# A planned schedule for a two-layer decoder trunk: weight loads placed by a rule of their own, new tables, and the last scalings as three tasks

## The chip, the cores and the metric

The kernel runs on one core of a Trainium2 chip. The metric is the device time of one execution in microseconds (us), lower is better. The core has a matrix engine (TensorE, PE in the rows; PEld are its weight loads), a vector engine (VectorE, DVE), a scalar engine (ScalarE, ACT), GpSimd (POOL) and SyncE (SP), which does no arithmetic and issues nearly all DMAs here. Each engine runs its own list of instructions in order and waits for the others through semaphores.

## The reference

Two layers over 256 tokens of width 1024, then a final RMSNorm, all in float32. Each layer is

```python
h = rms_norm(x, norm_g[layer])
proj = jnp.einsum('btd,dc->btc', h, w_in[layer])          # 1024 x 3584
sb_q, sb_k, sb_v, sb_g, mb_q, mb_k, mb_v, mb_g, mem_q, mem_g = jnp.split(proj, split_at, axis=-1)
o_sb = stick_breaking_attention(sb_q, sb_k, sb_v) * jax.nn.silu(sb_g)          # 6 heads of 64
o_mb = moba_attention(rotary(mb_q), rotary(mb_k), mb_v) * jax.nn.silu(mb_g)    # 6 heads; causal softmax at this length
mk, mv = jnp.split(rms_norm(mem, mem_norm_g[layer]) @ w_mem_kv[layer], 2, axis=-1)
o_mem = softmax_attention(mem_q, mk, mv) * jax.nn.silu(mem_g)                  # 4 heads, 256 memory tokens
x = x + jnp.concatenate([o_sb, o_mb, o_mem], axis=-1) @ w_out[layer]
```

Merging of heads is left out above. The weights of both layers are some 42 MB, and each is used once.

## The kernel before

**A planner writes the program.** The kernel is recorded by a small list scheduler (`Sched`). Every piece of work is a Python generator that yields requests `R(engine, need=..., alloc=...)`; the scheduler keeps a planned time for each engine, takes the request that can start first (priority breaks ties), and lets the generator emit its instructions. So the order on every engine is fixed when the program is built, from planned costs. On the chip an instruction waits only for its data and its buffers; the planned times are gone.

**Weights.** A layer's projections are pieces such as `sb_q`, `mb_k`, `mem_g`, `mk`, `mv` and the two halves `wo0`, `wo1` of the output projection; `ORDER` gives their sequence. A piece is cut into chunks of one to four K-tiles (`NK`, `NKP`). A chunk goes through three steps: a DMA on SP writes it into a ring `raw`; `hi_task` rounds it to a short float in `hl` (a CAST, nearly always ACT); `lo_task` subtracts to get the rest (`hl<-raw,hl`, DVE). PE then multiplies hi by hi, hi by lo and lo by hi, three matmuls, or two where the piece is in `DBL` (hi and lo side by side: one of double width and one). `KMAJ` pieces go through K outermost, the others finish one output chunk after another.

**What sets the order of the loads.** In the version before, the next load is emitted right after a `lo` step, as soon as the ring has room (`dma_room`).

**Attention.** Heads are taken in pairs. Scores are PE matmuls on 64 rows (`bank<-sb_k,sb_q`, `bank<-uT` for mb, `bank<-mem_k,mem_q`), here called row groups; `SCG` says which pairs go together. ACT and DVE make the weights `w`. The transposition goes by way of DRAM and is called a trip below: DVE transposes 32x32 blocks into `D`, SP dumps `D` to `Z` in DRAM and reads it back in another order (four DMAs, or eight for those in `HALVES`) into `F`, `T` or, for the rotated q and k of mb, `ga` and `uT`. The values are then applied by PE matmuls to 64 columns (`bank<-F,sb_v`, `bank<-T,mb_v`, `bank<-T,mv`): column groups, `PVG`. The rotation of mb (`rope_task`, then `rope_turn`) is one ACT copy `rn<-bank`, four small DVE operations on `ru` and `rn` and a transposition `D<-rn` for each of two halves of the tokens, before its trip.

**The end.** `out_task` scales each half of the tokens by its 1/rms in three parts, each followed by its store.

Of the kernel before, what the change touches and what calls it, by code (L numbers as in the profile page):

```python
# [9 lines left out]
BF = mybir.dt.bfloat16  # L10
AF = mybir.ActivationFunctionType
# [5 lines left out]
D = 1024  # L17
# [27 lines left out]
P_H0 = 28
P_RX = -442
P_M0 = -424
P_RM = 1289
P_M1 = -280
# [22 lines left out]
P_SILU = -378
SCG = (((("mb", 1), ("mb", 2), ("sb", 1)), (("mem", 0), ("mem", 1)), (("mb", 0),), (("sb", 2),), (("sb", 0),)),
       ((("mb", 0), ("sb", 1)), (("sb", 0), ("sb", 2)), (("mb", 2),), (("mem", 0), ("mem", 1)), (("mb", 1),)))
PVG = (((("mb", 1), ("sb", 1), ("sb", 0)), (("mb", 0), ("sb", 2)), (("mem", 0), ("mb", 2)), (("mem", 1),)),
       ((("mb", 1), ("mb", 2), ("sb", 0), ("mem", 1), ("mem", 0), ("sb", 1)), (("mb", 0), ("sb", 2))))
HOLD = 800.0
HALVES = [("F", 1, "sb", 2), ("F", 1, "mb", 0)]
CROWD = 2
SPARE1 = 4  # L80
# [3 lines left out]
DVE_W = -36995.9
AHEAD = 181
DVE_HI = 17839.2
SLACK_PE = 60.0
# [26 lines left out]
class Sched:  # L114
# [37 lines left out]
    def _avail(self, k, eng):  # L152
        r = k.req
        t = k.t
        if k.eng == eng:
            t += 0.0 if eng == "pe" else LAT_SAME
        elif k.eng:
            t += LAT_CROSS
        for n in r.get("need", ()):
            if n not in self.ready:  # L160
                return None
            t = max(t, self.ready[n])
        for tag in r.get("alloc", ()):
# [12 lines left out]
        return t + r.get("late", PE_LATE) if eng == "pe" and k.gen.__name__ != "main" else t  # L176
# [60 lines left out]
def hybrid_trunk(ctx: ExitStack, tc: tile.TileContext, x, mem, norm_g, w_in, w_mem_kv, w_out,  # L237
                 final_norm_g, xT, memT, gcols, consts, out):
    nc = tc.nc
# [3 lines left out]
    S = Sched()  # L243
# [38 lines left out]
    def act(out, in_, func=AF.Copy, **kw):  # L282
        c = 0.833 * _free(in_) + (50.0 if is_psum(in_) else 93.0)
        for a in ("scale", "bias"):
            if a in kw and not isinstance(kw[a], float):
                c += 93.0
        if "accum_out" in kw:
            c += 93.0
        if func == AF.Copy and not kw:
            nc.scalar.copy(out, in_)  # L290
        else:
            nc.scalar.activation(out, in_, func, **kw)  # L292
        S.op("act", c)
# [9 lines left out]
    def ts(out, a, s, op=OP.mult):  # L303
        nc.vector.tensor_scalar(out, a, s, None, op0=op)  # L304
        S.op("dve", 1.0417 * _free(out) + 65.0 if is_psum(a) else 0.52 * _free(out) + 130.0)
# [16 lines left out]
    xs = sb("xs", [128, 2, D])  # L322
# [6 lines left out]
    junk = sb("junk", [128, 512], BF)  # L329
# [71 lines left out]
    for l in range(DEPTH):  # L401
# [56 lines left out]
    rawp, hlp = places(RAWC), places(HLC)  # L458
# [655 lines left out]
    def out_task(t, nb):  # L1114
        r = ss[1, t][:, 7:8]
        yield from rstd(ss[1, t], nb, r)
        edge = (0, 512, 768, 1024) if nb == 3 else (0, 512, 1024)
        for eng, a, b, q in (("act", 640, D, nc.scalar if t else nc.sync), ("dve", 0, 256, nc.sync), ("dve", 256, 640, nc.sync)):
            yield R(eng, need=[("gain", n, t) for n in range(nb) if edge[n] < b and edge[n + 1] > a])
            s = xs[:, t, a:b]  # L1120
            if eng == "act":
                act(s, s, AF.Copy, scale=r)
            else:
                ts(s, s, r)
            q.dma_start(out_r[:, t, a:b], s)


    def main():
        hT, mT = Ts
        yield R("dve")  # L1130
        nc.vector.memset(junk, 0.0)
# [23 lines left out]
        for l in range(DEPTH):  # L1155
# [59 lines left out]
            if l == 0:  # L1215
                p = pieces["sb_qk", 0]
# [149 lines left out]
```

## Time and profile before

| | |
|---|---|
| three runs | 265.19, 265.92, 267.18 us; median 265.92 |
| the profiled execution | 265.58 us, of which the profile's span is 263.8 |
| busy | PE 97%, PEld 86%, DVE 85%, ACT 72%, POOL 2% |
| DMA | 67.05 MB, 254 GB/s on average |
| granted PE clock | 0.993 of full speed on average |
| chain that ended last | PE 87%, DMA 7%, ACT, DVE and SP 1% each |

Times in the rows are counted from the span's start. A row of the timeline has start, length, engine, line, operation, output<-input and the number of instructions merged into it. A matmul's length includes its latency; how much of PE it takes is read from the start of one to the start of the next. Line numbers are those of the kernel before; every operation is emitted by a helper, so the names of the tiles tell more than the line.

### The profile page before, as it was taken

The page shows a single profiled execution, that of the slowest core. Times are in us where ns is not written, and L with a number is a line of the kernel's source. Part 1 is how long each engine was busy: PE and PEld are TensorE (multiplying, and loading weights), DVE is VectorE, ACT ScalarE, POOL GpSimd, SP SyncE. Part 2 cuts the span into 40 slices and gives each one's busy share as a digit, 9 for nine tenths or more (in the row PEclk, how much of TensorE's full clock was granted, in tenths as well). Part 3 has the DMA queues.
Part 4 walks back from the last instruction along what each step waited for, and adds up shares of the span by engine and source line. Part 5 has one row for each costly group of instructions (what it writes and reads, how often), then busy time and mean ns, then how long its engine had stood idle before and what let it go on. Part 6 is the DMA issues. An engine that isn't in the chain of part 4 may idle for free.

```text
span 263.8 us, 4793 instructions
## 1 busy us (share of the span) xinstructions
PE 256.1 (97%) x1597; PEld 227.6 (86%) x1597; DVE 225.0 (85%) x517; ACT 190.2 (72%) x393; POOL 6.1 (2%) x18
## 2 busy tenths in 40 slices
PE   8999999999999999999999999999999999999990
PEld 5889999998899987878899998888898899787880
DVE  3878999999899999989799586999999995978353
ACT  4789995999698795967665272966897899356133
POOL 1002000000100000000000000000000000000000
PEclk9999999999999999999999999999999999999997
DMA  7999998989979999978955939599878996961004
GB/s 202 359 395 357 390 361 264 317 295 283 373 209 315 314 299 253 267 244 274 308 172 201 352 95 243 212 264 320 263 211 216 330 279 229 254 233 53 0 0 159
DMA packets 49880, 67.05 MB, mean 254 GB/s; under 512 B 4224, under 2 KB 41472, under 8 KB 49856
## 3 DMA queue, kind: packets, MB, share of 16 engines
q1 hardware_dynamic: 48912, 64.85, 77.4%
q0 software_dynamic: 512, 1.31, 1.7%
q10 hardware_dynamic: 432, 0.59, 0.7%
q8 instruction: 12, 0.20, 0.4%
q14 instruction: 12, 0.10, 0.1%
HBM read 57.29 MB, written 9.44 MB: 253 GB/s over the span
## 4 chain that ended last, share of the span: by engine, by line
PE 87%; DMA 7%; ACT 1%; SPq 1%; DVE 1%; issue 0%; DVEq 0%; ACTq 0%
PE bank L273 86%; DMA T<-Z 3%; DMA raw<-in_w_out_dram 3%; DMA raw<-in_w_in_dram 2%; PE bank L279 1%; SPq L1018 1%; ACT hl L290 1%; ACT junk L292 1%; DVE xs L296 1%; SPq L378 0%; DVE xs L304 0%; ACT ss L292 0%; DVE T L300 0%; DVEq L1362 0%; DVE ss L628 0%
## 5 line engine op out<-in xcount | busy, mean ns | idle before, releaser
L296 DVE TENSOR_TENSOR hl<-raw,hl 128x768 fp32r<-128x768 f32 (+5 forms) x107 | 99.6, 947 | 7.9 <-ACT hl L290 6.0
L273 PE MATMUL bank<-T,hl 128*128 128x256 f32 (+1 forms) x646 | 106.1, 322 | 0.2 <-DVE T L300 0.2
L273 PEld LDWEIGHTS bank<-T,hl 128*128 128x128 f32 x646 | 92.6, 189 | 11.7 <-issue 1.8
L290 ACT CAST hl<-raw 128x768 fp32r<-128x768 f32 (+5 forms) x105 | 85.3, 841 | 17.0 <-DMA raw<-in_w_in_dram 6.4
L273 PE MATMUL bank<-hl,T 128*128 128x384 f32 (+1 forms) x448 | 79.6, 335 | 0.0
L273 PEld LDWEIGHTS bank<-hl,T 128*128 128x128 f32 x448 | 76.5, 188 | 2.2 <-issue 0.3
L273 PE MATMUL bank<-hl,mxhi 128*128 128x512 f32 (+1 forms) x144 | 41.2, 367 | 0.0
L273 PEld LDWEIGHTS bank<-hl,mxhi 128*128 128x128 f32 x144 | 26.1, 189 | 4.9 <-issue 0.4
L273 PE MATMUL bank<-hl,mxlo 128*128 128x512 f32 (+1 forms) x72 | 26.3, 366 | 0.0
L877 DVE STREAM_TRANSPOSE D<-w 128x384 f32<-128x384 f32 (+1 forms) x32 | 19.2, 602 | 3.2 <-ACT w L292 2.9
L292 ACT ACTIVATE junk<-xs 128x512 bf16<-128x512 f32 (+1 forms) x12 | 7.3, 610 | 13.6 <-DVE xs L296 13.1
L273 PEld LDWEIGHTS bank<-hl,mxlo 128*128 128x128 f32 x72 | 13.6, 189 | 2.2
L292 ACT ACTIVATE T<-uT,gc 128x256 fp32r<-128x256 f32 x24 | 11.4, 506 | 2.7 <-DMA uT<-xT_dram 2.7
L810 DVE TENSOR_TENSOR_SCAN a<-a,a 128x256 f32<-128x256 f32 (+1 forms) x24 | 12.8, 539 | 0.1
L292 ACT ACTIVATE a<-bank 128x384 f32<-128x384 f32 x24 | 11.3, 483 | 1.6 <-DVE a L810 0.9
L292 ACT ACTIVATE w<-w,st 128x128 f32<-128x128 f32 (+1 forms) x24 | 10.7, 448 | 2.3 <-DVE st L830 2.2
L292 ACT ACTIVATE a<-a 128x384 f32<-128x384 f32 x24 | 11.8, 522 | 0.2
L300 DVE SCALAR_TENSOR_TENSOR T<-uT,gc,T 128x256 fp32r<-128x256 f32 x24 | 11.4, 476 | 0.6 <-ACT T L292 0.6
L304 DVE TENSOR_SCALAR w<-w,st 128x256 f32<-128x256 f32 (+1 forms) x40 | 11.2, 323 | 0.2
L296 DVE TENSOR_TENSOR xs<-bank,xs 128x512 f32<-128x512 f32 (+1 forms) x8 | 5.3, 656 | 6.6 <-PE bank L273 6.5
L292 ACT ACTIVATE w<-bank,st 128x256 f32<-128x256 f32 x16 | 7.4, 488 | 4.1 <-DVE st L843 4.1
L290 ACT COPY gT<-bank 128x256 f32<-128x256 f32 x10 | 3.6, 372 | 7.7 <-PE bank L273 7.7
(106 smaller groups left out, 218.6 us busy)
## 6 DMA issues: line engine op xcount, KB each, us to landing
raw<-in_w_in_dram SPq DMA_DIRECT2D x39, 384.0 KB, 4.8
Z<-D SPq DMA_DIRECT2D x16, 384.0 KB, 5.0
raw<-in_w_out_dram SPq DMA_DIRECT2D x8, 512.0 KB, 6.0
raw<-in_w_in_dram SPq DMA_DIRECT2D x18, 192.0 KB, 4.0
raw<-in_w_in_dram SPq DMA_DIRECT2D x6, 576.0 KB, 5.7
raw<-in_w_in_dram SPq DMA_DIRECT2D x13, 256.0 KB, 4.9
raw<-in_w_mem_kv_dram SPq DMA_DIRECT2D x6, 512.0 KB, 6.2
raw<-in_w_out_dram SPq DMA_DIRECT2D x4, 768.0 KB, 6.4
```

The source lines that it names most:

```text
L273: nc.tensor.matmul(out, lhsT=lhsT, rhs=rhs, start=start, stop=stop, **kw)
L279: nc.tensor.transpose(out, in_, idt)
L290: nc.scalar.copy(out, in_)
L292: nc.scalar.activation(out, in_, func, **kw)
L296: nc.vector.tensor_tensor(out, a, b, op=op)
L300: nc.vector.scalar_tensor_tensor(out, a, s, b, op0=op0, op1=op1)
L304: nc.vector.tensor_scalar(out, a, s, None, op0=op)
L810: nc.vector.tensor_tensor_scan(a[:, r0:r1], a[:, r0:r1], u[:, r0:r1], 0.0, OP.add, OP.add)
L877: nc.vector.transpose(o, w[:, :n * 128].rearrange("p (m j r) -> p m j r", j=4, r=32))
L1018: nc.sync.dma_start(Fv[32 * j:32 * j + 32, i0:i1], Zv.rearrange("(i r) (j e) -> j r i e", i=4, j=4)[j, :, i0:i1])
```

## The change

The weight loads get a task of their own. `load_task` emits load j when the ring has room and, in the plan, load j-6 has landed (`LOADS = 6`); its priority is ahead of everything (`P_LD`). This is a condition of the planner: it moves the DMA in SP's list, and adds no semaphore wait to it. Six loads (`SPLIT`) are issued as two DMAs of half the size. The tables are new: the sequence of pieces, their cuts (107 chunks become 125: layer 0 has 56 for 59, layer 1 has 69 for 48), which pieces are in `DBL` (`sb_g` of layer 0 comes in, `mem_q` of layer 0 goes out) and `KMAJ`, the groups of pairs, the priorities. The warm-up matmuls read a constant of ones that exists already in place of a tile that DVE cleared. `out_task` spawns its three scalings as tasks in place of emitting them one after another.

```diff
-KORD = ((2, 3, 0, 1, 4, 5, 6, 7), (4, 5, 6, 7, 0, 1, 2, 3))
+KORD = ((0, 1, 2, 3, 4, 5, 6, 7), (4, 5, 6, 7, 2, 3, 0, 1))
...
+SPLIT = (14, 30, 47, 49, 63, 78)
+LOADS = 6
+P_LD = -30388
...
-ORDER = (["sb_qk", "mb_k", "mem_q", "mb_q", "mk", "mb_v", "mv", "sb_v", "sb_g", "mb_g", "mem_g"], ["mk",
-         "mb_k", "mb_q", "mem_q", "sb_q", "sb_k", "mv", "mb_v", "mem_g", "mb_g", "sb_v", "sb_g"])
+ORDER = (["sb_qk", "mb_k", "mb_q", "mv", "mem_q", "sb_v", "mb_v", "mk", "sb_g", "mb_g", "mem_g"], ["mk",
+         "mb_q", "mb_k", "mem_q", "mv", "mem_g", "sb_k", "sb_q", "mb_v", "mb_g", "sb_v", "sb_g"])
...
-        for n in r.get("need", ()):
+        for n in (*r.get("need", ()), *r.get("after", ())):
...
         if j in SPLIT:
+            m = n // 2
+            dma(dst[:, one[0], one[1]], src[:, one[0], one[1]], None, q, now)
...
-            dma_room(S.cur.t)
+            if LOADS >= 20:
+                dma_room(S.cur.t)
+
+    def load_task():
+        while prog["dma"] < len(chunks):
+            j = prog["dma"]
+            yield R("sp", need=[("lo", max(rawp[j][1]))] if rawp[j][1] else [],
+                    after=[("raw", j - LOADS)] if j >= LOADS else [])
+            dma_chunk(S.cur.t)
...
     def out_task(t, nb):
         r = ss[1, t][:, 7:8]
         yield from rstd(ss[1, t], nb, r)
+        S.mark(("rstd", t))
+        for eng, a, b in (("dve", 0, 256), ("dve", 256, 640), ("act", 640, D)):
+            S.spawn(store_task(t, nb, r, eng, a, b), a // 256)
...
-        nc.vector.memset(junk, 0.0)
...
-            mm(acc[:, :n], junk[:, :128], junk[:, :n], True, True)
+            mm(acc[:, :n], nc.const_aps.tensor(1.0, [128, 128], BF), nc.const_aps.tensor(1.0, [128, n], BF), True, True)
```

Three places in layer 1 show what the new tables move. First PE, where the scores of two mb pairs are taken. Before, they stand alone (the two mem pairs have a row group of their own, one piece earlier):

```order
L273 MATMUL bank_94<-T_74,hl 128x256
L273 MATMUL bank_92<-uT 128x128
L273 MATMUL bank_90<-uT 128x128
L273 MATMUL bank_92<-uT 128x256
L273 MATMUL bank_90<-uT 128x256
L273 MATMUL bank_97<-uT 128x128
L273 MATMUL bank_93<-uT 128x128
L273 MATMUL bank_97<-uT 128x256
L273 MATMUL bank_93<-uT 128x256
L273 MATMUL bank_91<-T_74,hl 128x512
```

Of the change, PE at the same group, from the second mb pair on (the first stands just ahead):

```order
L277 MATMUL bank_94<-uT 128x128
L277 MATMUL bank_92<-uT 128x128
L277 MATMUL bank_94<-uT 128x256
L277 MATMUL bank_92<-uT 128x256
L277 MATMUL bank_93<-mem_k,mem_q 128x256
L277 MATMUL bank_95<-mem_k,mem_q 128x256
L277 MATMUL bank_93<-mem_k,mem_q 128x256
L277 MATMUL bank_95<-mem_k,mem_q 128x256
L277 MATMUL bank_91<-mem_k,mem_q 128x256
L277 MATMUL bank_97<-mem_k,mem_q 128x256
L277 MATMUL bank_91<-mem_k,mem_q 128x256
L277 MATMUL bank_97<-mem_k,mem_q 128x256
```

The two groups have become one, at the end of the piece `mem_g`. Ahead of it now stand `mb_q`, `mb_k`, `mem_q`, `mv` and `mem_g`; before, `mb_k`, `mb_q`, `mem_q`, `sb_q` and part of `sb_k`.

Second DVE, at the rotation of the mb piece that PE finishes last (before that is `mb_q`, now `mb_k`). `ru` and `rn` are the rotation's tiles, 117 and 118 those of the second half of the tokens, and `D_108` is what the trip takes. Before:

```order
L296 TENSOR_TENSOR hl<-raw,hl 128x768 x3
L296 TENSOR_TENSOR ru_118<-rn_117,cst 128x6x8
L296 TENSOR_TENSOR hl<-raw,hl 128x768
L296 TENSOR_TENSOR ru_118<-rn_117,cst 128x6x8
L296 TENSOR_TENSOR hl<-raw,hl 128x768
L296 TENSOR_TENSOR rn_117<-rn_117,cst 128x6x16
L296 TENSOR_TENSOR hl<-raw,hl 128x768
L296 TENSOR_TENSOR rn_117<-rn_117,ru_118 128x6x16
L296 TENSOR_TENSOR hl<-raw,hl 128x768
L300 SCALAR_TENSOR_TENSOR mem_q<-bank_95,mem_q 128x256
L300 SCALAR_TENSOR_TENSOR mem_q<-bank_96,mem_q 128x256
L986 STREAM_TRANSPOSE D_108<-rn_117 128x3x4x32
```

Of the change, DVE at the rotation of `mb_k`:

```order
L300 TENSOR_TENSOR ru_118<-rn_117,cst 128x6x8
L300 TENSOR_TENSOR hl<-raw,hl 128x256
L300 TENSOR_TENSOR rn_117<-rn_117,cst 128x6x16
L1004 STREAM_TRANSPOSE D_108<-rn_115 128x3x4x32
L300 TENSOR_TENSOR rn_117<-rn_117,ru_118 128x6x16
L300 TENSOR_TENSOR hl<-raw,hl 128x256
L1004 STREAM_TRANSPOSE D_108<-rn_117 128x3x4x32
L300 TENSOR_TENSOR hl<-raw,hl 128x256 x4
L300 TENSOR_TENSOR hl<-raw,hl 128x768
```

Four subtractions of 768 columns and two evacuations that stood between the second half's steps have gone behind the transposition; two subtractions of 256 columns remain.

Third SP, where the two mb trips of layer 1 are issued. `Z_112<-D_107` and `Z_113<-D_108` are the dumps of the first and the second piece, `uT<-Z` and `ga<-Z` the returns. Before:

```order
L1005 DMA Z_112<-D_107 128x768
L378 DMA raw<-in_w_in_dram 128x2x384
L378 DMA raw<-in_w_mem_kv_dram 128x4x256 x2
L1018 DMA uT<-Z_112 32x4x192 x4
L378 DMA raw<-in_w_in_dram 128x3x384 x2
L1005 DMA Z_113<-D_108 128x768
L1018 DMA ga_114<-Z_113 32x4x192 x4
L378 DMA raw<-in_w_in_dram 128x2x384
L1005 DMA Z_111<-D_107 128x1024
```

Of the change:

```order
L1023 DMA Z_112<-D_107 128x768
L382 DMA raw<-in_w_in_dram 128x2x384 x2
L382 DMA raw<-in_w_in_dram 128x384 x2
L1023 DMA Z_113<-D_108 128x768
L382 DMA raw<-in_w_in_dram 128x384
L1036 DMA ga_114<-Z_112 32x4x192 x4
L382 DMA raw<-in_w_in_dram 128x384 x5
L1036 DMA uT<-Z_113 32x4x192 x4
L382 DMA raw<-in_w_in_dram 128x3x384 x2
```

The second dump has 384, 384, 192 and 192 KB of weights just ahead of it in place of 512, 576 and 576 KB, and its returns stand behind five further loads.

More of the change, by code (lines that the diff above doesn't have):

```diff
@@ L28 @@
 NK = {256: 3, 384: 2, 512: 2, 768: 1}
-NKP = {("sb_k", 0): 3, ("sb_v", 1): 3, ("sb_g", 1): 4, ("mb_q", 1): 4, ("mb_k", 0): 1, ("mb_k", 1): 1, ("mb_v",
-       1): 3, ("mb_g", 1): 3, ("mem_q", 0): 2, ("mem_g", 0): 2, ("mem_g", 1): 2, ("mk", 0): 4, ("mk", 1): 4,
-       ("mv", 1): 4, ("wo0", 0): 3, ("wo0", 1): 3, ("wo1", 0): 3}
+NKP = {("sb_q", 0): 4, ("sb_q", 1): 1, ("sb_k", 0): 3, ("sb_v", 0): 1, ("mb_q", 1): 1, ("mb_k", 1): 4, ("mb_v",
+       1): 3, ("mb_g", 0): 4, ("mb_g", 1): 3, ("mem_g", 1): 1, ("mk", 1): 2, ("mv", 1): 4, ("wo0", 0): 3,
+       ("wo0", 1): 1, ("wo1", 0): 3, ("wo1", 1): 1}
 KSPLIT = (4, 4)
-KMAJ = (("sb_k", 1), ("sb_v", 1), ("sb_g", 0), ("mb_q", 0), ("mb_k", 0), ("mb_k", 1), ("mb_v", 0), ("mb_v", 1),
-        ("mb_g", 1), ("mem_q", 0), ("mem_q", 1), ("mem_g", 0), ("mk", 0), ("mv", 0))
+KMAJ = (("sb_k", 1), ("sb_v", 0), ("sb_v", 1), ("sb_g", 0), ("mb_q", 1), ("mb_k", 1), ("mb_v", 0), ("mem_q",
+        1), ("mem_g", 0), ("mem_g", 1), ("mv", 0), ("mv", 1))
 NTRIP = (0, 0)
-KORD = ((2, 3, 0, 1, 4, 5, 6, 7), (4, 5, 6, 7, 0, 1, 2, 3))
+KORD = ((0, 1, 2, 3, 4, 5, 6, 7), (4, 5, 6, 7, 2, 3, 0, 1))
 LAT_SAME, LAT_CROSS = 130.0, 240.0
@@ L41 @@
 COLD = 3900.0
-PRI = ({"sb": (-1494, -1070), "mb": (-780, -100), "mem": (-1672, -146)}, {"sb": (-38, -6), "mb": (-1502,
-       -1898), "mem": (-184, 522)})
+PRI = ({"sb": (-1480, -1786), "mb": (-1462, -476), "mem": (-2566, -538)}, {"sb": (-1100, -568), "mb": (-1520,
+       -3052), "mem": (-372, 932)})
 P_EV = -1047
[L45 to L49, printed above, removed]
+P_H0 = 1560
+P_RX = -530
+P_M0 = -1692
+P_RM = 827
+P_M1 = 198
 URG = 2
-X_AT = {5: 4, 6: 5, 9: 6, 10: 7}
-CST_AT = 14
-X0_AT = 9
+X_AT = {6: 4, 7: 5, 8: 6, 11: 7}
+CST_AT = 12
+X0_AT = 12
 X1_AT = 13
@@ L62 @@
 TRIP_LAT = 500.0
-ML_W = 0.0
-ML_T = 300.0
-ML_S = 200.0
+ML_W = 200.0
+ML_T = 0.0
+ML_S = 100.0
+SPLIT = (14, 30, 47, 49, 63, 78)
+LOADS = 6
+P_LD = -30388
 MEM_AT = 0
-ORDER = (["sb_qk", "mb_k", "mem_q", "mb_q", "mk", "mb_v", "mv", "sb_v", "sb_g", "mb_g", "mem_g"], ["mk",
-         "mb_k", "mb_q", "mem_q", "sb_q", "sb_k", "mv", "mb_v", "mem_g", "mb_g", "sb_v", "sb_g"])
+ORDER = (["sb_qk", "mb_k", "mb_q", "mv", "mem_q", "sb_v", "mb_v", "mk", "sb_g", "mb_g", "mem_g"], ["mk",
+         "mb_q", "mb_k", "mem_q", "mv", "mem_g", "sb_k", "sb_q", "mb_v", "mb_g", "sb_v", "sb_g"])
 NCH = {"sb": 3, "mb": 3, "mem": 2}
-SILU = ((("sb",), ("mb",), ("mem",)), (("sb",), ("mb", "mem")))
+SILU = ((("sb", "mb"), ("mem",)), (("sb",), ("mb",), ("mem",)))
 TABLE = 1290.0
[L72 to L80, printed above, removed]
+P_SILU = 160
+SCG = (((("mem", 0), ("mem", 1)), (("mb", 1), ("mb", 0), ("sb", 0)), (("sb", 2), ("sb", 1)), (("mb", 2),)),
+       ((("sb", 0), ("sb", 2), ("mb", 0)), (("mb", 2), ("mb", 1)), (("mem", 0),), (("sb", 1),), (("mem", 1),)))
+PVG = (((("mb", 0),), (("mem", 1), ("mem", 0)), (("sb", 2),), (("mb", 1),), (("sb", 1),), (("sb", 0),), (("mb",
+       2),)), ((("sb", 0), ("mem", 0), ("mem", 1), ("mb", 2), ("mb", 1)), (("sb", 2),), (("mb", 0),), (("sb",
+       1),)))
+HOLD = 9600.0
+HALVES = [("F", 0, "sb", 0), ("F", 1, "sb", 0), ("F", 1, "sb", 1)]
+CROWD = 153
+SPARE1 = 2
 SPARE2 = 1
-DBL = (("sb_qk", 0), ("sb_q", 1), ("sb_k", 1), ("sb_g", 1), ("mb_g", 1), ("mem_q", 0), ("mem_q", 1), ("mem_g",
+DBL = (("sb_qk", 0), ("sb_q", 1), ("sb_k", 1), ("sb_g", 0), ("sb_g", 1), ("mb_g", 1), ("mem_q", 1), ("mem_g",
        0), ("mem_g", 1), ("mk", 1), ("mv", 0), ("mv", 1))
[L84 to L87, printed above, removed]
+DVE_W = -7195.9
+AHEAD = 160
+DVE_HI = 42839.2
+SLACK_PE = 0.0
 SLACK = 0.0
@@ L479, in dma_chunk @@
         n = len(kk)
-        dma(raws(j).rearrange("p (k c) -> p k c", c=w),
-            p.src[:, kk[0]:kk[0] + n, c:c + w], ("raw", j), q, now)
+        dst, src = raws(j).rearrange("p (k c) -> p k c", c=w), p.src[:, kk[0]:kk[0] + n, c:c + w]
+        if j in SPLIT:
+            m = n // 2
+            one, two = ((slice(0, m), slice(0, w)), (slice(m, n), slice(0, w))) if m else ((slice(0, 1), slice(0, w // 2)), (slice(0, 1), slice(w // 2, w)))
+            dma(dst[:, one[0], one[1]], src[:, one[0], one[1]], None, q, now)
+            dst, src = dst[:, two[0], two[1]], src[:, two[0], two[1]]
+        dma(dst, src, ("raw", j), q, now)
         prog["dma"] += 1
@@ L535, in hybrid_trunk @@
     load_xT(3, 4)
-    dma_room()
+    if LOADS >= 20:
+        dma_room()
     def bcast_row(vec, name):
@@ L1116, in out_task, with store_task @@
         yield from rstd(ss[1, t], nb, r)
+        S.mark(("rstd", t))
+        for eng, a, b in (("dve", 0, 256), ("dve", 256, 640), ("act", 640, D)):
+            S.spawn(store_task(t, nb, r, eng, a, b), a // 256)
+    def store_task(t, nb, r, eng, a, b):
         edge = (0, 512, 768, 1024) if nb == 3 else (0, 512, 1024)
[L1118 to L1125, printed above, removed]
+        yield R(eng, need=[("rstd", t)] + [("gain", n, t) for n in range(nb) if edge[n] < b and edge[n + 1] > a])
+        s = xs[:, t, a:b]
+        if eng == "act":
+            act(s, s, AF.Copy, scale=r)
+        else:
+            ts(s, s, r)
+        (nc.scalar if t and eng == "act" else nc.sync).dma_start(out_r[:, t, a:b], s)
     def main():
@@ L1318, in hybrid_trunk @@
     S.spawn(lo_task(), urgent("lo"))
+    if LOADS < 20:
+        S.spawn(load_task(), P_LD)
     S.spawn(main(), 100)
```

## The prediction

> **What bounds the kernel now.** I read the busy shares first, then the waits, then the chain of work that ended last, then single stretches of it.
>
> ```profile
> PE 256.1 (97%) x1597; PEld 227.6 (86%) x1597; DVE 225.0 (85%) x517; ACT 190.2 (72%) x393; POOL 6.1 (2%) x18
> ```
>
> PE is busy for 97% of the span. Busy is not the same as unhindered, so the waits and the chain come next (a row of waits: total us, times, longest; a row of the chain: start, us, what).
>
> ```profile
> PE bank L273 <- DVE junk L1131: 1.2, 1, 1.2
> PE bank L273 <- DMA T<-Z: 0.3, 1, 0.3
> PE bank L273 <- DVE T L300: 0.2, 1, 0.2
> ```
>
> ```profile
> 106.69 7.95 DMA T<-Z
> ...
> 114.77 17.82 PE bank L273 x92
> ...
> 140.16 114.79 PE bank L273 x696
> ```
>
> These are all the waits that PE has: 1.2 us before its first instruction, 0.2 at the first real work and 0.3 in the middle, where a trip (the `T<-Z` of 106.69) is late. From 140.16 to the last matmul the chain is one row of PE. So everything that the change does to DVE, ACT, SP and the DMAs lies beside PE as long as it stays in time; only three kinds of thing can move the end: fewer or cheaper matmuls, the work behind the last of them, or a wait of PE that is new or gone.
>
> How dense PE is can be read from whole pieces in the timeline.
>
> ```profile
> 30.61 5.71 PE L273 MATMUL bank<-T,hl 128*128 128x512 f32 x32
> 36.16 8.50 PE L273 MATMUL bank<-hl,T 128*128 128x384 f32 x48
> ...
> 46.45 5.66 PE L273 MATMUL bank<-T,hl 128*128 128x256 f32 x45
> 51.95 8.31 PE L273 MATMUL bank<-hl,T 128*128 128x384 f32 x47
> ```
>
> A piece of 256 columns takes 5.55 us (30.61 to 36.16) with hi and lo side by side and 5.50 (46.45 to 51.95) without; one of 384 columns and 48 matmuls has a length of 8.50, or 177 ns a matmul, and another, 47 of it recorded, the same (8.31). Such pieces have no gaps in them that an order could take out.
>
> **The change part by part.** Base: the profiled execution, 265.58, which is 0.34 under the median of the runs (265.92).
>
> *Matmuls.* The two edits of `DBL` take one piece in and one out. By the two pieces of 256 columns above the forms differ by 0.05 us, so this is worth between -0.1 and +0.1; I take 0.
>
> *Groups.* Entering rows or columns costs PE time whatever the group holds, so fewer groups gain.
>
> ```profile
> 178.37 1.58 PE L273 MATMUL bank<-uT 64*128 64x128 f32 x16
> 179.88 1.66 PE L273 MATMUL bank<-T,hl 128*128 128x512 f32 x8
> 181.38 5.76 PE L273 MATMUL bank<-hl,T 128*128 128x512 f32 x32
> 187.07 0.93 PE L273 MATMUL bank<-uT 64*128 64x128 f32 x8
> ...
> 189.89 3.39 PE L273 MATMUL bank<-hl,T 128*128 128x384 f32 x18
> ```
>
> A group of two pairs takes 1.51 (178.37 to 179.88), one of four takes 2.82 (187.07 to 189.89): two of two would be 3.02, so a group that is joined to another saves 0.20. The change joins one. That is **-0.2**; its bounds are 0 (the mem pairs are matmuls of 256 columns and differ) and -0.4 (twice that).
>
> *Chunks.* 18 more. By form (count, then busy, mean ns):
>
> ```profile
> L296 DVE TENSOR_TENSOR hl<-raw,hl 128x768 fp32r<-128x768 f32 x41 | 38.6, 950 | 2.7 <-ACT hl L290 2.4
> ...
> L296 DVE TENSOR_TENSOR hl<-raw,hl 128x384 fp32r<-128x384 f32 x20 | 10.5, 554 | 1.8 <-ACT hl L290 1.5 <-PE bank L273 0.2
> ```
>
> ```profile
> L290 ACT CAST hl<-raw 128x768 fp32r<-128x768 f32 x41 | 33.8, 836 | 7.8 <-PE bank L273 3.1 <-DMA raw<-in_w_in_dram 2.9 <-issue 1.3
> ...
> L290 ACT CAST hl<-raw 128x384 fp32r<-128x384 f32 x18 | 8.6, 509 | 0.9 <-DMA raw<-in_w_in_dram 0.9
> ```
>
> A chunk of 768 that is cut in two costs DVE 2 x 554 - 950 = 158 ns and ACT 2 x 509 - 836 = 182 ns more: 18 of them 2.8 and 3.3 us. They fall in layer 1 (21 more there, 3 fewer in layer 0). How full is it there? (Columns: stretch, then busy us of PE, PEld, DVE, ACT, POOL with counts, PE clock, DMA share, GB/s.)
>
> ```profile
> 80.00:100.00 20.00, 20.00 (x165) 18.57 (x164) 19.98 (x57) 17.46 (x36) 0.00 (x0) 1.00 0.96 304
> 140.00:160.00 20.00, 20.00 (x118) 19.43 (x117) 15.47 (x33) 11.36 (x16) 0.00 (x0) 1.00 0.71 233
> 160.00:180.00 20.00, 20.00 (x126) 16.64 (x126) 17.88 (x42) 12.01 (x29) 0.00 (x0) 1.00 0.84 251
> ```
>
> DVE is full at 80 to 100 us, in layer 0, where no chunk is added and PE was not stopped even so. From 140 to 180 it leaves 4.5 and 2.1 us in 20. The 2.8 us over some 115 us of layer 1 are hidden by that: 0. Were that cover gone, they would cost up to 2.8.
>
> *Loads.* 24 more issues (18 chunks and 6 halves) and the new rule of when. (A row: count, KB each, median us from issue to landing.)
>
> ```profile
> raw<-in_w_in_dram SPq DMA_DIRECT2D x39, 384.0 KB, 4.8
> Z<-D SPq DMA_DIRECT2D x16, 384.0 KB, 5.0
> ...
> raw<-in_w_in_dram SPq DMA_DIRECT2D x18, 192.0 KB, 4.0
> ...
> raw<-in_w_out_dram SPq DMA_DIRECT2D x4, 256.0 KB, 6.6
> uT<-Z SPq DMA_DIRECT2D x8, 96.0 KB, 6.5
> ga<-Z SPq DMA_DIRECT2D x8, 96.0 KB, 2.9
> ```
>
> PE eats a piece of 256 columns (1024 KB of weights) in 5.55 us, 185 KB/us. Six loads of 192 KB in flight are 1152 KB; landing in 4.0 us they bring 288 KB/us. So six are enough as long as one of them lands in under 1152 / 185 = 6.2 us, and the DMA share of 0.71 and 0.84 where they are added leaves room: 0. What they cost if it doesn't hold is the second rival.
>
> The Trainium skill, "DMA: Bandwidth & Descriptors", section "Bandwidth", speaks against this part: DMAs should be batched to 1 MiB or more for three quarters of the peak. Our rows agree that small ones are dearer by the byte (192 KB in 4.0, 384 KB in 4.8); by the rule the sum would be that of the second rival, by the row of the DMA share it stays at 0.
>
> *The trip under the joined group.* The one new place where PE may wait. The group needs the second mb piece through rotation and trip, and PE now comes to it after `mem_q`, `mv` and `mem_g`. Before, the same chain ran like this:
>
> ```profile
> 155.10 7.83 PE L273 MATMUL bank<-T,hl 128*128 128x512 f32 x44
> ```
>
> ```profile
> 155.35 0.49 ACT L292 ACTIVATE rn<-bank 128x384 f32<-128x384 f32 x1 [0.72 <-ACT hl L290]
> ```
>
> ```profile
> 155.87 0.21 DVE L296 TENSOR_TENSOR ru<-rn,cst 128x48 f32<-128x48 f32 x1
> ...
> 159.50 0.26 DVE L296 TENSOR_TENSOR rn<-rn,ru 128x96 f32<-128x96 f32 x1
> ...
> 161.76 0.57 DVE L986 STREAM_TRANSPOSE D<-rn 128x384 f32<-128x384 f32 x1
> ```
>
> ```profile
> 162.35 0.34 SPq L1005 DMA_DIRECT2D Z<-D  x1
> 169.57 1.75 SPq L1018 DMA_DIRECT2D ga<-Z  x4
> ```
>
> PE ended the mb piece at 155.10 and started `mem_q`. In the change it reaches the group 5.55 (`mem_q`) + 5.69 (`mv`, 181.38 to 187.07) + 5.50 (`mem_g`) later, less some 0.3 as the first mb pair stands ahead of the piece's end: 171.5 on the old clock. The trip: ACT's copy ends at 155.84. Then DVE has, by the rows of the change's order, two `ru` and two `rn` (0.21, 0.21, 0.26, 0.26), two transpositions of 0.57 and two subtractions of 256 columns (some 0.45 each, an estimate below the 0.55 of 384): 158.8 in place of 162.33. The dump lands in 5.0 (median of `Z<-D`) to 7.2 (162.35 to 169.57, the one of before): 163.9 to 166.1. Four returns take 1.75 to issue: 165.7 to 167.9. They land in 2.9 (`ga`) to 6.5 (`uT`): 168.6 to 174.4. PE's wait is therefore between none (2.9 early) and 2.9. With the two medians for the same kind of dump and return, 5.0 and 6.5, it is 0.7; with 5.0 and the middle of `ga` and `uT`, 4.7, it is none. I take the middle of these, **+0.3**. Queued behind it on PE is all the rest of the layer, so a wait here is paid in full.
>
> The Trainium skill, "DMA: Bandwidth & Descriptors", section "Queues, rings and completion order", says that each DMA engine takes a ring's descriptors in order. By that the dump would take as long as what stands ahead of it in SP's list: 1152 KB now for 1664 before, so an estimate of 7.2 x 1152 / 1664 = 5.0 us, which is the lower end used above; that the old dump took 7.2 against a median of 5.0 agrees.
>
> *Other trips.* The wait of 0.3 at 114.77 may stay or go. The last trip of layer 1 was early before:
>
> ```profile
> 235.61 4.07 SPq L1018 DMA_DIRECT2D F<-Z  x8
> ```
>
> ```profile
> 242.52 0.87 PE L273 MATMUL bank<-T,mb_v 128*64 128x256 f32 x8
> ```
>
> Its returns are issued by 239.68, PE's group starts 2.8 later. I count 0 for these, with -0.3 and +0.5 as bounds.
>
> *Start and end.* The warm-up starts up to 1.2 earlier, but the first real matmuls wait for data, not for it, as the 0.2 on `T` shows: 0. The last scalings:
>
> ```profile
> 258.54 0.42 DVE L296 TENSOR_TENSOR xs<-bank,gb 128x256 f32<-128x256 f32 x1 [0.25 <-ACT junk L292]
> 258.88 1.00 DVE L304 TENSOR_SCALAR xs<-xs,ss 128x384 f32<-128x384 f32 x3
> ```
>
> They stand behind the last matmuls' result (`xs<-bank,gb`) and the last sum of squares, both there before and after; three tasks on the same two engines can trade places only, and the order of SP's stores with them: **-0.1**, between -0.3 and +0.2.
>
> Sum: 265.58 - 0.2 - 0.1 + 0.3 = **265.6**.
>
> **Rivals.**
>
> 1. *The joined group waits for its trip.* If dump and returns are as slow as the slowest rows, the wait is 2.9: 265.58 - 0.2 - 0.1 + 2.9 = 268.2, and between 266.3 and 268.8 for what lies between and for a second trip that is late. For it: the old dump took 7.2, and five more loads stand ahead of the returns. Against: less is queued ahead of the dump.
>
> 2. *Weights come late in layer 1: slower.* Two loads of 192 KB instead of one of 384 are 2 x 4.0 - 4.8 = 3.2 us more of one load's place in flight; 21 of them over six places are 21 x 3.2 / 6 = 11 us of feeding, over eight 8. If that bound PE, half of it would come through at the stretches of 0.84 and above: 4 us, 265.3 + 4 = 269.3. It decides from 6.2 us of landing on, which the row of 256 KB (6.6) passes and that of 192 KB (4.0) doesn't. The profile would show PE waiting for `hl`. Nothing of the kind stands in the waits now.
>
> 3. *It doesn't do what it says.* SP's place and the room in the ring set the loads before and after, and only the groups and the tail count: 265.3.
>
> 4. *Faster by more than 1%.* It would take 2.7 us from a PE whose waits, the first aside, are 0.5 and whose pieces are dense. No row offers it; what is left is what I can't see in the order: under 263.2.
>
> **How the numbers follow.** The forecast, 264.1 to 266.3, has 0.62. Rival 1 has 0.18, a third of it beyond 1%; rival 2 has 0.07; rival 3, 0.08, lies inside the forecast's range; rival 4 has 0.05. About 1% is what a measurement of this kernel can tell from no change, 2.7 us on 265.92: faster is below 263.3, slower above 268.6. So faster 0.05, slower 0.07 + 0.06 = 0.13, same 0.82. The range goes from the forecast's lower end (265.58 less the bounds 0.4, 0.3, 0.3 and 0.1 with no wait is 264.5, and the fastest run before, 265.19, lies another 0.4 under the profiled one: 264.1) to rival 1's slow end with the 0.3 by which the median lies above the profiled execution, 268.5; outside are rivals 2 and 4 and a little of rival 1, under 0.2.
>
> **What would show it.** Right: PE's waits in the changed profile under 1 us in all behind the start, the joined group starting within 1 us of the end of the matmuls ahead of it, the chain again nearly all PE, DVE a little less busy and ACT 2 to 3 us more. Rival 1: a wait of PE for `uT<-Z` near 171. Rival 2: waits for `hl` and ACT's CAST waiting for `raw`. The prediction would be wrong if PE waited at a place that was not looked at, since every trip and load has moved and only three were followed.

## The result and the profile after

The changed kernel takes 265.54 us (median of 18 runs, 263.88 to 271.89), the kernel before 266.29 in the same set. The ratio of the two is 0.9948, with a 95% interval of 0.9927 to 0.9968: some 1.4 us faster, within the 1% that the forecast called the same. (The ratio leaves out seven runs of the change from 268.0 to 271.9 that ran at a lower granted clock, so it lies below the quotient of the medians.)

The profiled execution of the change took 264.37 us, its span is 262.6 us. Its busy shares:

```profile
PE 255.7 (97%) x1589; PEld 226.8 (86%) x1589; DVE 224.5 (86%) x532; ACT 192.8 (73%) x413; POOL 5.9 (2%) x18
```

All waits of PE, and the long rows of the chain that ended last:

```profile
PE bank L277 <- PEq L1373: 0.8, 1, 0.8
PE bank L277 <- ACT T L296: 0.8, 1, 0.8
```

```profile
4.93 127.92 PE bank L277 x808
...
140.57 113.78 PE bank L277 x693
...
254.37 0.70 DVE xs L300
```

The 0.8 for `T` is the start; behind it PE waits for nothing, and the chain no longer passes a trip at 106 to 114 us. DVE does 15 more instructions in 0.5 us less, ACT 20 more in 2.6 us more, the signs that the prediction named for being right.

Where the 1.2 us between the two profiled executions come from is read by cutting each into four: to the start of the first real matmul, from there to the start of the last, from there to the span's end, and what lies outside the span. These are the last matmul and the stores of before and then of the change, in the timeline:

```profile
257.53 0.28 PE L273 MATMUL bank<-hl,mxhi 128*128 128x256 f32 x1
...
258.17 2.50 SPq L1125 DMA_DIRECT2D out_dram<-xs  x5
```

```profile
256.92 0.28 PE L277 MATMUL bank<-hl,mxhi 128*128 128x256 f32 x1
256.92 0.61 ACT L296 ACTIVATE xs<-xs,ss 128x384 f32<-128x384 f32 x1
257.12 2.59 SPq L1147 DMA_DIRECT2D out_dram<-xs  x5
```

| us | before | change | change again (first experiment) |
|---|---|---|---|
| first real matmul starts | 4.57 | 4.93 | 4.72 |
| from there to the start of the last | 252.96 | 251.99 | 252.61 |
| from there to the span's end | 6.27 | 5.68 | 5.67 |
| outside the span | 1.78 | 1.77 | 1.75 |
| sum | 265.58 | 264.37 | 264.75 |

The span is known to 0.1 us only, so the last two rows before the sum are too.

**The end** gives 0.59. Before, SP has issued its five stores 258.17 + 2.50 - 257.53 = 3.14 us behind the start of the last matmul; now 2.79. That is 0.35. The other 0.24 lies behind the issues, and the landing of a store is at most 0.1 of it (1.9 to 2.5 us from issue to landing before, 1.9 to 2.4 now); what the rest is stays open.

**The stretch of matmuls** gives 0.97. Taken matmul by matmul (the time from one start to the next, less the usual one of its form), 5.5 us of before are gaps, 4.6 of the change. Three differ: a row group less, 0.39; the wait for the `T<-Z` trip at 114.5 (a gap of 0.41, now 0.09), 0.32; and a gap at 7.15 us in the start, 0.39 to 0.09, 0.30, which the later first matmul gives back. The two edits of `DBL` are worth 0.05 to 0.1 by their counts. Of the three only the row group is the change's: a profile of the kernel before with nothing but the new end (the third experiment) has PE's list as it was and no wait at this trip either.

```profile
114.68 1.08 PE L273 MATMUL bank<-T,mv 128*64 128x256 f32 x8
```

So the 0.3 is scatter of the first profile.

**The joined group** stands where the sum put it:

```profile
166.17 5.37 PE L277 MATMUL bank<-T,hl 128*128 128x512 f32 x30
171.47 1.58 PE L277 MATMUL bank<-uT 64*128 64x128 f32 x16
172.89 1.89 PE L277 MATMUL bank<-mem_k,mem_q 64*128 64x256 f32 x16
174.71 1.55 PE L277 MATMUL bank<-T,hl 128*128 128x256 f32 x7
```

PE comes to it at 171.47 and goes on without a wait. Its trip: on DVE the last transposition, in SP's list the dump of the second piece and its returns, and how long those returns took to land:

```profile
157.64 0.57 DVE L1004 STREAM_TRANSPOSE D<-rn 128x384 f32<-128x384 f32 x1
```

```profile
158.24 0.33 SPq L1023 DMA_DIRECT2D Z<-D  x1
...
164.42 1.85 SPq L1036 DMA_DIRECT2D uT<-Z  x4
```

```profile
DMA to landing us min/median/max: 4.8/4.9/4.9
```

The last of the four returns is issued at 165.8 and lands at 170.7: 0.8 us early.

### The profile page after: what moved, and what is told of

The parts are those of the page before. It is cut to its first block, busy times and chain, and to the rows that moved or that the text cites. A ratio compares the mean times of both kernels' runs of the same rounds, so it can differ in the third digit from the quotient of the medians.

```text
span 262.6 us, 4894 instructions
## 1 busy us (share of the span) xinstructions
PE 255.7 (97%) x1589; PEld 226.8 (86%) x1589; DVE 224.5 (86%) x532; ACT 192.8 (73%) x413; POOL 5.9 (2%) x18
## 4 chain that ended last, share of the span: by engine, by line
PE 95%; ACT 1%; DMA 1%; DVE 0%; issue 0%; SPq 0%; DVEq 0%; ACTq 0%
PE bank L277 94%; DMA uT<-xT_dram 1%; PE bank L283 1%; ACT junk L296 1%; ACT ss L296 0%; DVE xs L300 0%; ACT T L296 0%; SPq L382 0%; DVE xs L308 0%; ACT xs L296 0%; DVEq L1385 0%; ACTq L296 0%
## 5 line engine op out<-in xcount | busy, mean ns | idle before, releaser
L300 DVE TENSOR_TENSOR hl<-raw,hl 128x768 fp32r<-128x768 f32 (+6 forms) x125 | 101.2, 830 | 8.5 <-ACT hl L294 7.7
L277 PE MATMUL bank<-T,hl 128*128 128x512 f32 (+1 forms) x638 | 105.4, 324 | 0.8 <-ACT T L296 0.8
L294 ACT CAST hl<-raw 128x768 fp32r<-128x768 f32 (+6 forms) x123 | 87.1, 745 | 11.4 <-PE bank L277 7.0
L294 ACT COPY gT<-bank 128x256 f32<-128x256 f32 x13 | 4.7, 371 | 6.9 <-PE bank L277 6.8
```

Source lines behind the costliest of these rows:

```text
L277: nc.tensor.matmul(out, lhsT=lhsT, rhs=rhs, start=start, stop=stop, **kw)
L300: nc.vector.tensor_tensor(out, a, b, op=op)
```

## Experiments

The theory after the comparison (T in the texts) was that the gain is the sum of these small things: the end, the row group, the one wait that is gone. The rivals were that the profile had caught a lucky end, and that the rule for the loads is the gain in itself. "Before" in a ratio is always the kernel before in the same set of runs.

### The change again, and the end on either side

> The changed kernel once more, on the same chip as the next three. Theory T (the gain is a sum of three small things: some 0.6 us in the work behind the last matmul, 0.4 from the joined row group, 0.3 from the one wait of PE for a T<-Z trip that is gone): ratio to before 0.993 to 0.997, tail from the start of the last matmul to the span's end 5.6 to 5.8 us, PE without a wait over 0.2 us behind its first real matmul. Rival R (the tail of the first profile was luck of the DMAs): tail between 5.7 and 6.4.

265.10 us (12 runs, 263.93 to 266.04), ratio 0.9959 (0.9937 to 0.9981). The end again takes 5.67 us. PE has gaps of 0.28 and 0.14 in the first 10 us, which the first profile did not have (T had allowed 0.2), and 0.17 at a place that is taken up below.

```diff
-        S.mark(("rstd", t))
-        for eng, a, b in (("dve", 0, 256), ("dve", 256, 640), ("act", 640, D)):
-            S.spawn(store_task(t, nb, r, eng, a, b), a // 256)
+        for eng, a, b, q in (("act", 640, D, ...), ("dve", 0, 256, nc.sync), ("dve", 256, 640, nc.sync)):
+            yield R(eng, need=[...])
```

> The change with the old out_task (scalings one after another, ACT's first). T: the tail goes back to 6.2 to 6.3 us and the time is 0.4 to 0.6 us above that of the change. By the prediction's term for the end: 0.1 us, tail unchanged within 0.1.

265.23 us, ratio 0.9958 (0.9934 to 0.9981): no difference that the times can show. In the profile SP's stores are issued by 3.15 us behind the start of the last matmul, as before the change, and the whole end takes 6.04. T had expected 6.2 to 6.3 and 0.4 to 0.6 us of time: both missed.

The same edit the other way round, on the kernel before:

> The kernel before with the new three scaling tasks alone. T: tail 5.6 to 5.8 us in place of 6.27, time 0.4 to 0.6 us under before (ratio about 0.998). By the prediction's term: 0.1 us under before.

265.28 us, ratio 0.9977 (0.9956 to 0.9998), the 0.6 us that T expected, but with an interval from 0.05 to 1.2. The stores are issued by 2.78 us, as in the change; the whole end takes 5.94, not T's 5.6 to 5.8. So in the profiles the new end brings the last store's issue 0.35 us forward, put in and taken out; the times show it put in, at the edge of the noise, and not taken out. With the new end the rest of the tail was shorter in seven profiles (5.65 to 5.68) and not in four others (5.94 to 6.12), so beyond 0.35 nothing is shown. The prediction's 0.1 was too small by the profiles, the 0.59 of the first profile partly luck.

### The old warm-up

```diff
+        nc.vector.memset(junk, 0.0)
...
-            mm(acc[:, :n], nc.const_aps.tensor(1.0, [128, 128], BF), ...)
+            mm(acc[:, :n], junk[:, :128], junk[:, :n], True, True)
```

> The change with the old warm-up (DVE clears a tile, the matmuls read it). T and the prediction: first real matmul at 4.6 to 4.9 us as with the change, since ACT's T and the DMA ahead of it set it; time within 0.2 us of the change. Rival: the earlier warm-up is worth what it starts earlier, 0.4 us (1.19 to 0.78), so 0.4 us slower than the change.

265.17 us, ratio 0.9967 (0.9935 to 0.9999): the same as the change. The first real matmul starts at 5.30, later than in any other profile, yet the matmuls then take 251.94. T's 4.6 to 4.9 missed, but what starts late there runs without the early gaps: PE's first row group starts at 48.4 us, in the two profiles of the change at 48.2 and 48.5. The earlier warm-up is worth nothing that shows.

### The rule and the tables, each without the other

```diff
-LOADS = 6
+LOADS = 20
```

> The change with the old rule for the loads (emitted right after a lo step as soon as the ring has room); tables, cuts and splits as changed. The planner moves other work too. T: the rule only keeps loads from standing in SP's list ahead of trips; without it PE gets waits for T<-Z, F<-Z or uT<-Z of 0.5 to 3 us in all, time 266 to 268. Rival N (loads are limited by the ring and SP anyway, the rule does nothing): SP's list nearly the same in its effect, time within 0.5 us of the change.

283.53 us, ratio 1.0652 (1.0615 to 1.0689), far more than expected. In SP's list, loads now stand ahead of trips at the end of layer 0 (start, length, what):

```profile
109.99 1.11 SPq L382 DMA_DIRECT2D raw<-in_w_out_dram  x2
111.14 3.53 SPq L382 DMA_DIRECT2D raw<-in_w_mem_kv_dram  x4
114.72 0.93 SPq L382 DMA_DIRECT2D raw<-in_w_in_dram  x2
115.93 2.31 SPq L1036 DMA_DIRECT2D T<-Z  x4
119.29 4.30 SPq L382 DMA_DIRECT2D raw<-in_w_in_dram  x7
123.64 0.43 SPq L1023 DMA_DIRECT2D Z<-D  x1
128.32 1.93 SPq L1036 DMA_DIRECT2D T<-Z  x4
```

In the change the same two trips' returns go out as one row, eight from 105.67 on, and those loads behind them. PE pays:

```profile
120.08 0.50 PE L277 MATMUL bank<-hl,mxhi 128*128 128x512 f32 x1 [2.62 <-ACT mxhi L294]
...
132.35 1.55 PE L277 MATMUL bank<-T,mb_v 128*64 128x256 f32 x8 [6.73 <-DMA T<-Z]
...
137.07 1.06 PE L277 MATMUL bank<-hl,mxhi 128*128 128x512 f32 x2
137.92 0.63 PE L277 MATMUL bank<-hl,mxlo 128*128 128x512 f32 x1
...
140.28 0.62 PE L277 MATMUL bank<-hl,mxhi 128*128 128x512 f32 x2
```

Its waits behind the start are 12.0 us in all. Part of the rest is in the rows around the longest wait: from 137.07 to 137.92 two matmuls take 0.43 each, from 140.28 on 0.23. The windows of this run show why (us, then PE, PEld, DVE, ACT, POOL busy, clock, DMA share, GB/s):

```profile
120.00:122.40 2.40, 1.72 (x9) 0.90 (x11) 2.40 (x6) 0.55 (x2) 0.00 (x0) 1.00 1.11 209
122.50:139.40 16.90, 8.98 (x31) 5.36 (x28) 4.24 (x11) 0.00 (x0) 0.00 (x0) 0.50 0.33 103
```

The granted clock is 0.50 from 122.5 to 139.4 us and 1.00 on either side: it fell before the wait of 6.73, behind waits of 2.62 and 0.59. The edit isn't pure either. The planner cut the groups otherwise, seven on 64 rows and eight to 64 columns in place of five and five, some 2 us by an estimate of 0.39 a group.

The other half: the code of the change with the tables of before and no split loads.

```diff
-NKP, KMAJ, ORDER, SCG, PVG, DBL, PRI, ... (of the change)
+NKP, KMAJ, ORDER, SCG, PVG, DBL, PRI, ... (of before)
-SPLIT = (14, 30, 47, 49, 63, 78)
+SPLIT = ()
```

> The code of the change (rule with six ahead, new end, new warm-up) with all tables of before and no split loads. T: the tables were fitted to the old rule, so with the new one the trips fall elsewhere: 0.6 us gained at the end, 0 to 2 us lost in new waits of PE: 265 to 267.5. Rival G (the rule itself is the gain): under 265, with no wait of PE for T<-Z.

275.67 us, ratio 1.0379 (1.0339 to 1.0420), again outside both expectations. One trip near the end is late: its returns stand behind four loads in SP's list.

```profile
227.27 3.26 SPq L381 DMA_DIRECT2D raw<-in_w_out_dram  x4
230.63 2.24 SPq L1035 DMA_DIRECT2D F<-Z  x4
```

The matmuls behind the wait are slow for 3.6 us:

```profile
239.57 0.87 PE L276 MATMUL bank<-F,sb_v 128*64 128x256 f32 x8 [4.05 <-DMA F<-Z]
...
241.98 1.05 PE L276 MATMUL bank<-hl,mxhi 128*128 128x512 f32 x2
242.84 0.63 PE L276 MATMUL bank<-hl,mxlo 128*128 128x512 f32 x1
...
245.11 0.61 PE L276 MATMUL bank<-hl,mxhi 128*128 128x512 f32 x2
```

The granted clock over that stretch, 1.00 on either side:

```profile
240.90:244.20 3.30, 3.30 (x8) 2.25 (x9) 3.30 (x13) 0.00 (x0) 0.00 (x0) 0.50 0.41 96
```

The other waits of this run behind the start make 2.3 us, and there are seven row and six column groups in place of six and five. So the rule is no gain in itself, nor are the tables: either half alone loses 10 to 18 us against the kernel before. "The loads: 0" in the sum holds for the pair only.

### Smaller loads

```diff
+        for o, i in halves(dst, src) if <a whole weight load of layer 1> else ((dst, src),):
-        (q or nc.sync).dma_start(dst, src)
+            (q or nc.sync).dma_start(o, i)
```

> The change with every weight load of layer 1 (67 that were whole) issued as two DMAs of half the size; the order on every engine and the planner's numbers stay as they are, only SP issues 67 more DMAs. T: there is room in the DMA queues and on SP, PE is fed: within 0.5 us of the change. The prediction's second rival (small DMAs make weights late): 67 loads in place of 21 at 3.2 us of a load's place each, so 4 us and more above the change, ACT's CAST waiting for raw, PE for hl.

267.42 us, ratio 1.0055 (1.0022 to 1.0087). By the ratios that is 2.5 to 2.8 us over the change, between the two expectations. PE's waits say which part is the edit's:

```profile
PE bank L277 <- DVE mxlo L300: 1.9, 1, 1.9
PE bank L277 <- PEq L1380: 0.8, 1, 0.8
PE bank L277 <- DMA uT<-Z: 0.4, 1, 0.4
```

PE never waits for `hl`, so small DMAs did not make weights late. The 0.4 (two gaps of 0.7 in all beyond the usual) is at the joined group: SP issues twice as many loads ahead of its returns, which go out at 170.51 in place of 164.42, and the 0.8 us of margin are gone. The 1.9 stand at 106.7 us, and the first halved load comes behind that in SP's list; a profile below has a wait of 1.1 at the same place without halved loads. So it is most likely not the edit. Its chain:

```profile
97.78 8.14 DMA raw<-in_w_out_dram
...
106.03 1.47 ACT hl L294
107.50 0.31 ACT mxhi L294
```

The same load of 768 KB was issued at 97.39 in the profile of the change and had landed by 103.8; here it landed at 105.9. ACT's CAST waits for it, behind that CAST in ACT's list stands the rounding of `mxhi`, and PE's first `mxlo` needs it (`mxhi` and `mxlo` are hi and lo of the gated attention output, which the output projection takes). Whether all of the difference is this place and the trip is not shown; in this profile the two make 2.6 of the 3.3 to 3.7 us by which it lies above those of the change, and a longer end behind SP's last store 0.4.

### The margin of the joined group

```diff
+            if (l, name, t) == (1, "mb_k", 1):
+                for _ in range(8):
+                    nc.vector.tensor_scalar(rn[0], rn[0], 1.0, None, op0=OP.mult)
             nc.vector.transpose(o, rn[0].rearrange(...))
```

> The change with eight multiplications by 1.0 of rn (128x384) on DVE just ahead of the last transposition of mb_k in layer 1; the order on all engines stays as it is else. It makes the dump under the joined group some 2.4 us later (8 x 0.3). T: the last return of that trip lands about 0.8 us before PE comes to the group at 171.5 (issue 165.8, landing 4.9), so PE waits 1.4 to 1.8 us there and the time goes up by as much. Rival: landing is hidden further (the wait ends on something else), no wait, time within 0.3 us of the change.

265.98 us, ratio 1.0018 (0.9982 to 1.0053): 1.6 to 1.9 us over the change by the ratios (1.0018 against 0.9959 and 0.9948). The delay, the returns and the group:

```profile
157.70 3.12 DVE L1006 TENSOR_SCALAR rn<-rn 128x384 f32<-128x384 f32 x8
```

```profile
167.16 1.85 SPq L1039 DMA_DIRECT2D uT<-Z  x4
```

```profile
172.33 0.46 PE L277 MATMUL bank<-uT 64*128 64x128 f32 x2 [0.73 <-DMA uT<-Z]
173.04 1.54 PE L277 MATMUL bank<-uT 64*128 64x128 f32 x14 [0.25 <-DMA uT<-Z]
```

The returns go out 2.74 later (167.16 against 164.42), land 0.5 sooner (4.4 for 4.9), and PE waits 1.0. So the margin was 2.74 - 0.5 - 1.0 = 1.2, near the 0.8 read from the trace. T had the wait at 1.4 to 1.8 and the time up by as much: the wait is shorter, and why the time went up by more than the wait is not shown. The trip that the first rival named is real, with about one us in hand.

### The place at the end of layer 0

```diff
-        copy(mxhi[:, k, :], m, e)
+        if <the first that ACT takes in layer 0>:
+            nc.vector.tensor_copy(mxhi[:, k, :], m)
+        else:
+            copy(mxhi[:, k, :], m, e)
```

> The change with one instruction moved: the first mxhi CAST that ACT does at the end of layer 0, behind the CAST of a 768 KB piece of w_out, is done by DVE next to its two neighbours; nothing else moves. In the profiles so far the load ahead of that CAST landed 6.4 to 8.1 us after its issue, and PE stood up to 2.1 us at its first mxlo for it. T: PE's first mxlo no longer hangs on the load: no excess at that place, time 0 to 0.5 us under the change (ratio to before 0.993 to 0.996) and a narrower spread of the runs. Rival: the place is not what spreads the runs: same time, and the wait moves to the next mxlo or to hl of w_out.

264.42 us (12 runs, 263.66 to 266.55; ten of them between 263.66 and 264.67), ratio 0.9949 (0.9925 to 0.9973). That is faster than before, by as much as the change within the intervals (0.9948 and 0.9959); the closer runs fit the theory, but that it beats the change is not shown. In its profile ACT still waits for the load, and DVE goes on without it:

```profile
103.64 2.00 ACT L294 CAST hl<-raw 128x1536 fp32r<-128x1536 f32 x2 [0.76 <-DMA raw<-in_w_out_dram]
```

```profile
104.74 0.28 DVE L294 CAST mxhi<-ev 128x256 fp32r<-128x256 f32 x1
104.94 0.49 DVE L315 CAST mxhi<-ev 128x256 fp32r<-128x256 f32 x2
105.34 1.09 DVE L300 TENSOR_TENSOR mxlo<-ev,mxhi 128x256 fp32r<-128x256 f32 x3
```

There is no gap at PE's first `mxlo`, and the span, 262.3, is the shortest of the profiles. But the load landed in 6.0 us here, and with 6.3 the first profile of the change had no gap either. So this profile shows that the path by way of the load is cut, not that time is gained by it.

### The group taken apart, the splits undone

```diff
-((("sb", 0), ("sb", 2), ("mb", 0)), (("mb", 2), ("mb", 1)), (("mem", 0),), (("sb", 1),), (("mem", 1),))
+((("sb", 0), ("sb", 2), ("mb", 0)), (("mb", 2), ("mb", 1)), (("mem", 1), ("mem", 0)), (("sb", 1),))
```

> The change with the joined row group of layer 1 taken apart again (the mem scores in a group of their own, ahead of mem_g). The planner moves what follows from it. T: one more row group costs 0.4 us of PE by the gaps around a group in the trace (about 0.09 + 0.10 going in and the same coming out): 0.4 above the change if no new wait comes with it, up to 2 with one. The prediction's step: 0.2.

266.21 us, ratio 0.9995 (0.9965 to 1.0025), 1.0 to 1.2 us over the change by the ratios. Its profile has three row groups in layer 1 with 0.39 of gaps each, where the change has two. It also has a wait at the place above, which the edit does not touch:

```profile
PE bank L277 <- DVE mxlo L300: 1.1, 1, 1.1
```

The load ahead of it took 7.1 us. So the 0.4 rest on the gaps, not on the time.

```diff
-SPLIT = (14, 30, 47, 49, 63, 78)
+SPLIT = ()
```

> The change with the six split loads whole again (SPLIT empty); the order on PE, DVE and ACT changes in a handful of places only. T and the prediction: 0 within 0.5 us. Rival: the splits bring the first chunks of a piece in time, 0.5 to 2 us above the change, with ACT's CAST waiting longer for raw.

265.49 us, ratio 0.9984 (0.9962 to 1.0005). By the ratios 0.7 to 1.0 us over the change, with intervals that overlap. The profile has 0.36 at the place above, 0.2 at 13.8 us and no other new gap. What the splits are worth, between 0 and 1 us, stays open.

## Why the prediction was right, and where its sum was off

The forecast was 265.6 and no change that a measurement can tell; the measured median is 265.54. That the two agree to 0.1 us is luck: the kernel before came out at 266.29 beside it, so the sum of the terms, which was 0.0, should have been -1.1 to -1.4. What is shown, the row group (0.39), the end (0.35) and `DBL` (up to 0.1), makes some 0.8; the rest is not accounted for. Point by point:

- **What bounds the kernel** holds. PE ran dense and the change moved it by tenths. The split chunks cost what was worked out: by the counts and means of the pages the subtractions on DVE take 125 x 830 - 107 x 947 ns = 2.4 us more and the roundings on ACT 123 x 745 - 105 x 841 = 3.3. All of it lay beside PE, and DVE's total still fell by 0.5, as other operations left it.
- **Groups, -0.2: too small by half.** The mem group of before, in the timeline:

```profile
162.86 2.00 PE L273 MATMUL bank<-mem_k,mem_q 64*128 64x256 f32 x16
164.78 6.60 PE L273 MATMUL bank<-T,hl 128*128 128x512 f32 x36
```

The step took a group's price from its own start to the start of what follows. By those rows the joined group saves 0.19 too: 1.51 and, for the mem group before, 1.92, against 174.71 - 171.47 = 3.24. Two of the four gaps lie outside that stretch, 0.09 ahead of the first matmul of the group and 0.10 behind the first that follows. With all four it is 0.39. (Shown by the gaps of the trace; the run with the group taken apart has them back, its time can't tell 0.4.)
- **The trip under the joined group, +0.3: it was 0.** PE's arrival was forecast at 171.5 and came at 171.47; the transposition's end at 158.8 came at 158.21. The returns landed in 4.9, near the middle of `ga` and `uT`. By that, the lower of the two cases, there is no wait, and half of the other should not have been added. That the returns went out at 164.42, in the forecast's stretch of 163.9 to 166.1, is luck, for two steps were off. The dump, forecast at 5.0 to 7.2 us, took 3.1:

```profile
DMA to landing us min/median/max: 3.1/3.1/3.1
```

It had landed at 161.3, and the returns stood for another 3.1 us behind five loads in SP's list (161.33 to 164.38), a stretch that the sum has no term for. The Trainium skill's page "DMA: Bandwidth & Descriptors", section "Queues, rings and completion order", says that each DMA engine consumes the descriptors of a ring in order. The trace agrees with that order: the dump landed 1.0 us behind the load just ahead of it, before (168.6 and 169.6 us) and now (160.4 and 161.3). It doesn't agree with the 5.0 that the prediction scaled from it, since the list does not tell what is still in flight: the first of the four loads that were counted ahead of the dump had landed when it was issued, at 157.4, and two more landed by 159.4.
- **Other trips, 0 with -0.3 as a bound: 0 is borne out.** The wait at 114.77 is not in the profile of the change, but not in that of the kernel before with the new end either.
- **The end, -0.1 with -0.3 as a bound: -0.35 by SP's issues.** "Three tasks on the same two engines can trade places only" overlooked that the first half of the tokens has its stores ahead of the last matmuls' result: its scalings are no longer behind ACT's, so SP starts on its five stores 0.20 us behind the start of the last matmul in place of 0.64, and is through with them 0.35 sooner.
- **Loads and chunks, 0:** right for the change as a whole, and resting on more than the text said. It argued from room in the DMAs. In the two runs that undo one half of the change, PE's longest waits are for trips whose dump (the wait of 6.73 us) or returns (4.05) stand behind loads in SP's list. With the old rule the same tables lose 18 us, though no more bytes move.
- **Rival 1** (the trip) was the nearest: a margin of 0.8 to 1.2 us. **Rival 2** (small loads) is refuted at three times the number of extra loads as far as weights go. The Trainium skill's page "DMA: Bandwidth & Descriptors", section "Bandwidth", says to batch DMAs to 1 MiB and more for three quarters of the peak. No run here shows that peak to be needed: with the halved loads the DMA share was 0.67 to 0.93 between 120 and 220 us, and PE did not wait for weights. What they cost was SP's time ahead of a trip. **Rival 3** (only groups and the end count) came closest to what the profiles show of the gain, but its ground, that the rule does nothing, is refuted.
- **Overlooked:** the CAST of `mxhi` behind a load at the end of layer 0. The prediction followed three places and said that others could decide; this is one, worth 0 and 0.17 us in the two profiles of the change and up to 1.9 in those of its variants.

## What to carry to other kernels

Where one engine is dense and another issues all DMAs in one list, ask of a new load rule not how many bytes it moves but what it puts ahead of each return in that list, and how early that return lands; write the margin down for each. Where a plan follows from rule and tables together, undoing one half measures a third kernel, not that half's worth. And an instruction on the critical path that stands in its engine's list behind one that waits for a DMA inherits that DMA's scatter; moving a 0.3 us operation to a neighbour takes it off that path, though a gain in time was not shown here. Last, take a wait of 0.3 us in a single profile for scatter until a second one has it.

## What the runs showed of the hardware

A wait of PE can cost more than itself. After the wait of 4.05 us (tables of before under the new rule) the matmuls of 512 columns took 0.43 us in place of 0.23 for the next 3.6 us, at a granted clock of 0.50 from 240.9 to 244.2 us. With the old rule the clock was 0.50 from 122.5 us on, behind waits of 2.62 and 0.59 with one matmul between them, through the wait of 6.73 and for 7 us of broken work behind it. After single waits of 0.7 to 1.9 us in the other profiles the matmuls took the usual time at once. The Trainium skill's page "TensorE: Matmul & The Clock Gate", section "What's actually happening", says that the clock goes to half after an idle window of some 3.4 us and back after as long a busy one. The runs here agree in the factor and, after the wait of 4.05, in the length of the slow stretch; how long PE must idle they do not fix.

The same load of 768 KB, at the same place in SP's list, took from 5.5 us (the change with the old end) to 8.14 (halved loads) to land from one profile to another. A margin under the 2.6 us between them, at such a place, is spread in the times, not safety.
